# A shorter softplus chain and a new written order in a one-core hybrid decoder layer

## The chip, the cores and the metric

The kernel runs on one core of a Trainium2 chip. The metric is the device time of one execution in microseconds (us). A core has a matmul engine (PE; PEld is its weight load), a vector engine (DVE), an activation engine (ACT), GpSimd (POOL), and DMA queues, of which SP's carries the plain loads and stores and POOL's the accumulating ones. SBUF is the working memory, PSUM the memory that matmuls write.

## The reference

One layer on x of 1024 tokens by 1024 channels, in float32. `h` is x after an RMS norm, scaled and shifted by a modulation vector `mod`; the product of `h` with W_in gives five groups of 1024 columns each. The core of it:

```python
mod = c_act @ mod_w[l] + mod_b[l]
shift, scale, gate = jnp.split(mod, 3, axis=-1)
h = rmsnorm(x, norm_g[l]) * (1.0 + scale[:, None, :]) + shift[:, None, :]
u = h @ w_in[l]
cv, cg, cs, lx, ls = jnp.split(u, [D_CONV, 2 * D_CONV, 3 * D_CONV, 3 * D_CONV + D_LRU], axis=-1)
v = cv * jax.nn.sigmoid(cg)
v = causal_depthwise_conv(v, dw_w[l], dw_b[l])           # 31 taps
v = jax.nn.silu(layernorm(v, cln_g[l], cln_b[l]))
y_conv = (v @ pw2_w[l] + pw2_b[l]) * jax.nn.silu(cs)
xs = causal_depthwise_conv(lx, sc_w[l], sc_b[l])         # 4 taps
r = sigmoid(xs @ wr + br); i = sigmoid(xs @ wi + bi)     # block-diagonal, 8 heads
log_a = -LRU_C * r * jax.nn.softplus(-lam[l])
a = jnp.exp(log_a)
hs = linear_scan(a, jnp.sqrt(-jnp.expm1(2.0 * log_a)) * (i * xs))
y_lru = hs * jax.nn.silu(ls)
x = rmsnorm(x + (1.0 + gate) * (concat(y_conv, y_lru) @ w_out[l]), final_g)
```

The softplus of `lam` is a vector of 1024 numbers, held as 128 x 8. The `exp`, `tanh` and `sqrt` steps of every head's gates need it, from head 0 on.

## The kernel before

Everything is kept with channels on the 128 partitions and the 1024 tokens along a row, so a tile is 128 x 1024. A float32 operand is split into two rounded parts, `hi` and `lo` (in names: `uh`/`ul` for the input, `whi`/`wlo` for weights, `yh`/`yl` for the results y), and a product is three matmul passes, hi by hi, lo by hi and hi by lo. `whi` is an ACT cast of the loaded `raw`; `wlo` is `raw - whi`, made on DVE, on POOL or by an accumulating DMA.

W_in is worked off in column blocks of 128, called slots and numbered n. A slot n is 48 matmuls of 128 x 512 (8 row blocks k, 3 passes, 2 halves) into a PSUM tile `ps<n>`; there are three such tiles, taken in turn, so a slot can begin when the tile of three before has been read. What a slot computes is given by the string ORDER: `i4` is a CG or CV block and so on, `g1` the six-matmul gate products of head 1 (`gate1_0`, `gate1_1`), `i28+i36` a pair of blocks done together with fewer products (`up`, `dn`). Behind a slot its tile is read out: CG by a sigmoid on ACT (`sig`), CV by a product with `sig` on DVE (`v`, line 561), CS by a SiLU on ACT (`scs`, then stored to DRAM), LS by a SiLU on ACT (`sls`), LX by four taps on ACT and DVE (`xs`). `gates(i, n)` (from line 1419) turns the gate products into `r` and `g`, `a`, the scan `r` and the result `sls<i>*r`, which is y of the head. It is split at once or, for heads in the list YSP, stored to DRAM (`yd`) and fetched again (`yr`) ahead of the products that use it.

The 31 taps of the convolution run as fillers: on DVE for most tiles (`cacc`, `caccs`, sums in PSUM), as ACT products added by POOL's DMAs for tiles 1 and 3 (`cq`, `co`, `es`, `oo`). The pair slots need sums and differences of the input blocks, made on POOL (`hx`, `hls`). `modw` steps on DVE multiply a modulation weight by the silu of c and sum it.

Behind the slots come the first products with W_out (`lp`, `lx`, `ly` and so on, from the y of the lru heads), the layer norm, the products with pw2, the rest of W_out, the final norm and the stores. `lp0` is the first that reads `yh5` and `yl5`.

The order of the instructions on each engine is fixed when the program is built. A class Plan takes every operation with a priority and an estimated cost, plays the engines against each other with the limits of buffers, and writes down the order in which it would start them. The numbers at the top of the file (SPP the priority of the softplus, YRES the buffers kept back for fetches, PYM and PXL and others the heads whose products are given to POOL) and the table TURNS, which shifts single operations by a few units, set that order. On the chip each engine works its list strictly from the front.

`softplus8` (from line 1213) evaluates softplus as a series: with s = u / (u + 2) the logarithm's odd series is a polynomial in s2 = s * s, built from the highest term by a product (TT, line 561) and an addition (TS, line 575) for each term. Its eight-column steps have the name `sp_q`.

Of the kernel before, what the change touches and what calls it, by code (L numbers as in the profile page):

```python
# [14 lines left out]
P = 128  # L15
D = 1024
T = 1024
# [17 lines left out]
ORDER = "i10 i24 i2 g0 i25 i11 i3 i26 i12 i33 i4 g1 i34 i23 g2 i13 i35 i5 i27 g3 i21 i14 i39 i6 i28+i36 i15 i30+i38 i7 i29+i37 g5 i31 g4 i19 i18+i22 g7 g6 i20"  # L35
# [46 lines left out]
SPN = 40  # L82
# [10 lines left out]
DUOA = 3  # L93
DUOW = "big"
YSP = (0, 1, 2, 3)
YRES = 5
TSP = 24
# [3 lines left out]
DENG = {15: ("POOL", "DVE", "DMA"), 16: ("DVE", "DMA", "POOL"), 17: ("DMA", "DMA", "DVE"), 18: ("DMA", "DMA", "POOL"), 20: ("DMA", "DVE", "POOL"), 21: ("DVE", "POOL", "DVE"), 23: ("POOL", "POOL", "DMA"), 24: ("DMA", "DVE", "POOL"), 27: ("POOL", "DMA", "POOL"), 29: ("DMA", "DMA", "POOL"), 30: ("DVE", "DVE", "DVE"), 31: ("POOL", "DMA", "DVE"), 32: ("POOL", "POOL", "DMA"), 34: ("DMA", "DVE", "DVE"), 35: ("POOL", "POOL", "DVE"), 39: ("DVE", "POOL", "DVE"), 41: ("POOL", "DMA", "POOL")}  # L101
YDMA = (1, 3, 4, 6, 7)
EVD = 0
DUOE = 0.6
# [8 lines left out]
YSTEP = 0.3  # L113
LTD = (2,1)
PREN = 5
PRES = 4
PREP = 18
XCP = 17
PLAND = 8.0
XCN = 28  # L120
XCS = 1
LEV = ()
LWB = "big"
LWO = 0.7
FINP = -0.5
# [8 lines left out]
FORKN = -200  # L134
# [5 lines left out]
LSN = 2  # L140
# [8 lines left out]
LRV = (0, 1, 2, 3, 4, 6)  # L149
# [13 lines left out]
SPP = 35  # L163
# [5 lines left out]
WE = {5: "POOL", 6: "DMA", 7: "DVE", 8: "POOL", 10: "DVE", 11: "POOL", 12: "POOL", 14: "DMA", 18: "DVE", 19: "DVE", 20: "DVE", 23: "DVE", 24: "DVE", 25: "POOL", 26: "DVE", 27: "DVE", 28: "DMA", 30: "POOL", 32: "DMA", 34: "POOL", 35: "DVE", 37: "DVE", 38: "DVE", 39: "DMA", 41: "DMA"}  # L169
PDIRECT = (0, 2, 5, 6)  # L170
D1S = {19: -1.35, 21: -0.3, 32: -1.35, 33: 0.0, 35: -1.35, 36: -1.35, 38: 0.0, 39: -1.35, 40: 0.0, 41: -1.35}
PGM, PYM, PXL, PYL, PXR = (2, 3, 7), (4,), (0,), (1, 4), (4, 6)
# [19 lines left out]
    ("ACT", "c3", "es3", 0): 2,  # L192
    ("ACT", "graw3", "ghi3", 0): 0.9,
    ("ACT", "graw6", "ghi6", 0): -4,
    ("ACT", "raw36", "whi36", 0): -5.7,
    ("ACT", "rawpw21_0", "whipw21", 0): 2.6,
    ("ACT", "v1", "co1_12", 0): -5.4,
    ("ACT", "v3", "co3_4", 0): 0.7,
    ("ACT", "v6", "caccs6", 0): -0.1,
    ("ACT", "wz37", "wsh37", 0): 2,  # L200
    ("DVE", "c3", "mean", 0): -2.3,
    ("DVE", "c3", "vt1", 0): -2,
    ("DVE", "c3", "vu1", 0): 1,
    ("DVE", "c6", "mean", 0): -0.9,
    ("DVE", "c6", "vla3", 0): 1.1,
    ("DVE", "c6", "vu3", 0): 7.1,
    ("DVE", "c7", "lnbc", 0): 2.6,
    ("DVE", "cr1", "mean", 0): -1.9,
    ("DVE", "cr1", "vlb0", 0): 1.7,
    ("DVE", "cr1", "vt0", 0): 2.1,  # L210
    ("DVE", "cr2", "mean", 0): -5.5,
    ("DVE", "cr4", "lnbc", 0): 2,
    ("DVE", "vu1", "vla1", 0): 2.3,
    ("DVE", "yu0", "ylT40", 0): 0.3,
    ("PE", "fhi6", "first0", 2): 4,
    ("PE", "ghi6", "gate6_1", 0): -2,
    ("PE", "h34pw21", "xpw2_1", 7): 1.8,
    ("PE", "h34pw21", "ypw2_1", 0): -0.2,
    ("PE", "h34pw21", "ypw2_1", 1): -0.2,
    ("PE", "h34pw21", "ypw2_1", 2): -0.2,  # L220
    ("PE", "hlpw21", "xpw2_1", 0): 2,
    ("PE", "hlpw22", "xpw2_2", 0): 0.2,
    ("PE", "lsh3", "ld3", 0): 1.7,
    ("PE", "lsh3", "lx3", 2): -0.3,
    ("PE", "lsh3", "lx3", 3): -0.3,
    ("PE", "whi18", "ps18", 0): -1.2,
# [24 lines left out]
    ("PE", "whipw20", "xpw2_0", 1): 0.2,
    ("PE", "whipw20", "xpw2_0", 2): 5.2,
# [237 lines left out]
def hymba_layer(ctx: ExitStack, tc: tile.TileContext, xT, vecs, mod_w, w_first, w_in,  # L490
# [1041 lines left out]
    def acc_store(n, m, t):  # L1532
        ADD(n + 0.5, lambda: acc_d[m], t, r=[t, ("accd", m)], w=[("accd", m)], flight=LAND)
# [193 lines left out]
    def duo(m0, m1, n):  # L1727
# [14 lines left out]
        for to, (a, ai, ak), (b, bi, bk) , op in (  # L1742
# [4 lines left out]
            TT(q, CSUB, block(z, to), block(a, ai), block(b, bi), op, w_, r=ak + bk, w=[(z, to)],  # L1747
# [92 lines left out]
    def after_start(n):  # L1840
# [8 lines left out]
        if 0 <= (n - XCN) // XCS < KT and (n - XCN) % XCS == 0:  # L1849
            x_copy((n - XCN) // XCS, [started[n]])  # L1850
# [291 lines left out]
```

## Time and profile before

| | us |
|---|---|
| three runs | 729.41, 724.18, 729.10 |
| median | 729.1 |
| profiled execution | 728.72 |
| its span, first to last instruction | 726.7 |

| engine | busy us | share of the span |
|---|---|---|
| PE | 713.7 | 98% |
| PEld | 594.0 | 82% |
| DVE | 651.4 | 90% |
| ACT | 477.8 | 66% |
| POOL | 218.8 | 30% |

The profiled execution is 2.02 us longer than its span; a sum made from the trace's rows is set against 728.72. In the timelines a row gives the start, the duration, the engine, the line and the names with their numbers left out, and in brackets the idle time ahead of it and what ended it. Consecutive alike instructions are drawn together (x2). Rows of one engine overlap by their pipeline, so the cost of an instruction is the distance between starts.

### The profile page before, as it was taken

To read this page: it belongs to the slowest core of one execution; us is meant where nothing else is said; L and a number is where in the kernel's file an instruction comes from. 1 tells how busy PE (TensorE), PEld (TensorE's weight loads), DVE (VectorE), ACT (ScalarE), POOL (GpSimd) and SP (SyncE) were. 2 spreads that over 40 slices of the span, in tenths; PEclk is the share of its full clock that TensorE was granted. 3 is DMA by queue.
4 is the path that set the end of the run, shared out by engine and by line. 5 is a ranking of instruction groups with operands and counts; after the bars stand their busy time and mean duration, and the time that the engine had idled before them with its cause. 6 is when DMAs were issued, how large, how long until landed. Compare 5 with 4: busy or idle time off the path is not lost.

```text
span 726.7 us, 9084 instructions
## 1 busy us (share of the span) xinstructions
PE 713.7 (98%) x3244; PEld 594.0 (82%) x3244; DVE 651.4 (90%) x890; ACT 477.8 (66%) x604; POOL 218.8 (30%) x189
## 2 busy tenths in 40 slices
PE   9999999999979999999999999999999999999995
PEld 8888888888868888888888888878888888888885
DVE  7989999999999989989989999798799765998747
ACT  7650687868766693984694879946697644755322
POOL 0023334533676642463254262200101101010001
PEclk9999999999989999999999999999999999999999
DMA  9936357997976989879946328996838745783106
GB/s 345 407 143 191 56 154 199 229 259 173 194 171 165 235 228 243 203 184 250 221 121 198 86 72 218 268 303 157 223 82 194 205 104 130 230 228 128 52 1 231
DMA packets 45052, 135.95 MB, mean 187 GB/s; under 512 B 5088, under 2 KB 14560, under 8 KB 44896
## 3 DMA queue, kind: packets, MB, share of 16 engines
q0 software_dynamic: 16848, 45.52, 35.2%
q1 hardware_dynamic: 27152, 88.95, 34.6%
q10 hardware_dynamic: 1008, 0.92, 0.4%
q8 instruction: 25, 0.41, 0.2%
q14 instruction: 19, 0.16, 0.1%
HBM read 83.17 MB, written 25.17 MB: 149 GB/s over the span
## 4 chain that ended last, share of the span: by engine, by line
PE 68%; DVE 22%; ACT 6%; issue 3%; POOL 1%; DVEq 0%; ACTq 0%
PE ps L694 21%; PE xpw L870 6%; PE xout L870 6%; PE first L1003 5%; DVE caccs L553 4%; PE ypw L870 3%; DVE cacc L553 3%; PE lx L1578 3%; PE dn L1778 2%; PE up L694 2%; DVE xs L553 2%; PE gate L1429 1%; PE zpw L870 1%; PE lx L694 1%; PE dn L694 1%
## 5 line engine op out<-in xcount | busy, mean ns | idle before, releaser
L694 PE MATMUL ps<-uh,whi 128*128 128x512 f32 x448 | 139.3, 392 | 4.2 <-DVE v L561 4.2
L694 PE MATMUL ps<-uh,wlo 128*128 128x512 f32 x448 | 138.8, 391 | 0.0
L694 PE MATMUL ps<-ul,whi 128*128 128x512 f32 x448 | 138.8, 391 | 0.0
L694 PEld LDWEIGHTS ps<-uh,whi 128*128 128x128 f32 x448 | 84.7, 190 | 22.2 <-issue 4.6
L694 PEld LDWEIGHTS ps<-ul,whi 128*128 128x128 f32 x448 | 84.7, 189 | 17.8
L694 PEld LDWEIGHTS ps<-uh,wlo 128*128 128x128 f32 x448 | 84.7, 189 | 17.7
L553 DVE SCALAR_TENSOR_TENSOR cacc<-v,V,cacc 128x511 f32<-128x511 f32 (+14 forms) x90 | 67.0, 744 | 0.4
L542 ACT ACT_TABLE_LOAD x47 | 60.3, 1283 | 9.6 <-DVE r L1441 7.8
L561 POOL TENSOR_TENSOR wlo<-raw,whi 128x1024 fp32r<-128x1024 f32 (+1 forms) x16 | 41.2, 2580 | 78.4 <-ACT whi L534 76.3
L553 DVE SCALAR_TENSOR_TENSOR caccs<-v,V,caccs 128x511 f32<-128x511 f32 (+6 forms) x84 | 62.6, 746 | 1.9 <-ACT caccs L542 0.7
L553 DVE SCALAR_TENSOR_TENSOR caccs<-c,wsum,caccs 128x511 f32<-128x511 f32 (+6 forms) x84 | 62.4, 742 | 0.5
L534 ACT CAST whi<-raw 128x1024 fp32r<-128x1024 f32 (+1 forms) x44 | 44.0, 1007 | 23.8 <-PE ps L694 11.4
L566 POOL DMA_DIRECT2D es<-cq x30 | 29.1, 970 | 44.9 <-DMA es<-cq 10.8
L553 DVE SCALAR_TENSOR_TENSOR modw<-modw,sc 128x1024 f32<-128x1024 f32 x23 | 34.1, 1485 | 0.0
L566 POOL DMA_DIRECT2D oo<-co x26 | 27.6, 1060 | 18.2 <-DMA oo<-co 5.0
L542 ACT ACTIVATE cq<-v,V 128x511 f32<-128x511 f32 (+14 forms) x30 | 21.3, 711 | 10.8 <-DVE v L561 4.2
L561 POOL TENSOR_TENSOR o<-fin,bc 128x256 f32<-128x256 f32 (+1 forms) x6 | 4.9, 830 | 70.8 <-ACT bc L534 70.8
L561 DVE TENSOR_TENSOR wlo<-raw,whi 128x1024 fp32r<-128x1024 f32 (+1 forms) x21 | 26.2, 1246 | 0.0
L566 POOL DMA_DIRECT2D lz<-in_w_out_dram x16 | 14.1, 996 | 37.1 <-ACT lz L542 29.8
L566 POOL DMA_DIRECT2D accd<-acc x8 | 7.3, 910 | 58.5 <-ACT acc L542 34.2
L542 ACT ACTIVATE finsq<-fin 128x512 f32<-128x512 f32 (+2 forms) x14 | 7.9, 570 | 23.1 <-DVE fin L553 15.4
L1441 DVE TENSOR_TENSOR_SCAN r<-a,xs 128x1024 f32<-128x1024 f32 x8 | 22.4, 2796 | 0.1
(525 smaller groups left out, 1937.5 us busy)
## 6 DMA issues: line engine op xcount, KB each, us to landing
raw<-in_w_in_dram SPq DMA_DIRECT2D x36, 512.0 KB, 4.2
modw<-in_mod_w_dram SPq DMA_DIRECT2D x24, 512.0 KB, 8.0
scsd<-scs SPq DMA_DIRECT2D x8, 512.0 KB, 3.1
raw<-in_w_out_dram SPq DMA_DIRECT2D x8, 512.0 KB, 4.6
accd<-acc POOLq DMA_DIRECT2D x8, 512.0 KB, 7.2
rawpw<-in_pw_dram SPq DMA_DIRECT2D x8, 512.0 KB, 4.8
scsr<-scsd SPq DMA_DIRECT2D x8, 512.0 KB, 5.1
rawout<-in_w_out_dram SPq DMA_DIRECT2D x8, 512.0 KB, 3.7
```

The source lines that it names most:

```text
L534: act.copy(out(), in_())
L542: act.activation(out=out(), in_=in_(), func=func, **kw)
L553: dve.scalar_tensor_tensor(out=out(), in0=in0(), scalar=scalar, in1=in1(), op0=op0, op1=op1, accum_out=accum)
L561: lambda: e.tensor_tensor(out=out(), in0=a(), in1=b(), op=op), prio, r, w,
L566: return S.op("POOL", ISSUE, lambda: pool.dma_start(out(), a(), accum_op=ALU.add), prio, r, w, lag=RATE * n / T, after=after, flight=flight)
L694: pe.matmul(ps()[:, a - off:b - off], k3(lhs)()[:, at, :], rhs[k]()[:, a:b], start=(k == first and lhs is wh and rhs is xh and (a - off) % ...
L870: pe.matmul(half(ps, 0)(), half(*lhs)()[:, j * P:j * P + P], half(*rhs)(), start=start and at == 0 and i == 0, stop=at == len(order) - 1 a ...
L1003: pe.matmul(ps()[:, a - off:b - off], fw_part(lhs, k, i * P, i * P + P)(), rhs()[:, a:b], start=k == 0 and lhs is wh and rhs is xh, stop=k ...
L1429: pe.matmul(ps()[:, c0:c1], lhs()[:, j, :], rhs()[:, c0:c1], start=st == 0, stop=st == 2)
L1441: S.op("DVE", 2.2, lambda: dve.tensor_tensor_scan(out=r(), data0=a(), data1=xs(), initial=0.0, op0=ALU.mult, op1=ALU.add), pr, [a, xs], [r])
L1578: pe.matmul(half(ps, h)(), lhs()[:, o:o + P], half(*rhs)(), start=begin and at == 0 and t == 0, stop=at == len(order) - 1 and t == len(ter ...
L1778: pe.matmul(half(ps, h)(), lhs()[:, o:o + P], half(rhs, z)(), start=begin and j == 0 and t == 0, stop=j == NJ - 1 and t == 2, skip_group_c ...
```

## The change

Three things are done together.

The softplus chain. The product and the addition of a term become one instruction, `(q + 1/n) * s2`, so fifteen steps become eight:

```diff
-        TS(pr, q, s2, 1.0 / 17.0, 1.0 / 15.0, ALU.mult, ALU.add, r=[s2], w=[q])
-        for n in (13, 11, 9, 7, 5, 3, 1):
-            TT(pr, "DVE", q, q, s2, ALU.mult, KT, r=[q, s2], w=[q])
-            TS(pr, q, q, 1.0 / n, None, ALU.add, r=[q], w=[q])
-        TT(pr, "DVE", q, q, s, ALU.mult, KT, r=[q, s], w=[q])
+        TS(pr, q, s2, 1.0 / 17.0, None, ALU.mult, r=[s2], w=[q])
+        for n in (15, 13, 11, 9, 7, 5, 3):
+            STT(pr, q, q, 1.0 / n, s2, ALU.add, ALU.mult, KT, r=[q, s2], w=[q])
+        STT(pr, q, q, 1.0, s, ALU.add, ALU.mult, KT, r=[q, s], w=[q])
...
-SPP = 35
+SPP = -20
```

The settings of the planner, cut to those that move something named here, and two lines for the table of turns:

```diff
-ORDER = "i10 i24 i2 g0 i25 i11 i3 i26 i12 i33 i4 g1 i34 i23 g2 i13 i35 i5 i27 g3 i21 i14 i39 i6 i28+i36 i15 i30+i38 i7 i29+i37 g5 i31 g4 i19 i18+i22 g7 g6 i20"
+ORDER = "i10 i24 i2 g0 i25 i11 i3 i26 i33 i12 i4 g1 i34 i23 g2 i13 i35 i5 i27 g3 i20 i14 i39 i6 i28+i36 i15 i30+i38 i7 i29+i37 g5 i31 g4 i19 i18+i22 g6 i21 g7"
...
-YSP = (0, 1, 2, 3)
+YSP = (0, 1, 2, 3, 5)
...
-LRV = (0, 1, 2, 3, 4, 6)
+LRV = (0, 1, 2, 3, 4, 5, 6)
...
-PGM, PYM, PXL, PYL, PXR = (2, 3, 7), (4,), (0,), (1, 4), (4, 6)
+PGM, PYM, PXL, PYL, PXR = (2, 3), (0, 4), (0,), (4, 6, 7), (4, 6)
...
-    ("PE", "whi18", "ps18", 0): -1.2,
...
+    ("DVE", "v4", "caccs4", 0): -0.6,
```

Of the new helpers and choices in the code (a reload of the input from DRAM for the pair slots, other engines for their sums, another way to keep x for the end) the settings leave all off. The entries of the table WE for slots 27, 31, 33, 34, 40 and 41 have no effect, since those are pair slots or products of W_out, which other tables govern.

In instructions: PE has the same matmuls. DVE has six rows fewer: the seven softplus steps, and sls0's product goes to POOL (PYM), while head 7's product of `g` and `xs` comes from POOL (PGM) and one `wlo` of 768 columns is more. ACT loads its tables twice less often. POOL has one DMA fewer. SP has two DMAs more: y of head 5 is stored and fetched (512 KB each). Two neighbouring slots, a CG block and an LS block, change places (slots 14 and 15).

The softplus steps, which stood one by one among the taps and the `xs` steps from 100 to 121 us of the profile, stand right behind the last `ul` products now, one between each two of `wlo7`, `glo0`, `glo1`, `wsum`, `c0` and `bias2`, ahead of nearly all taps.

The first place: DVE ahead of `v4`, the read-out of slot 16, near 206 us. Before:

```order
L553 SCALAR_TENSOR_TENSOR caccs2_1549<-v2_1197,V_80,caccs2_1549 128x500
L553 SCALAR_TENSOR_TENSOR caccs2_1549<-v2_1197,V_80,caccs2_1549 128x499
L553 SCALAR_TENSOR_TENSOR modw17_1765,macc_96<-modw17_1765,sc_175 128x1024
L561 TENSOR_TENSOR v4_1849<-ps16_1745,sig4_1679 128x1024
L561 TENSOR_TENSOR wlo18_1853<-raw18_1713,whi18_1838 128x1024
L561 TENSOR_TENSOR xs1_1314<-g1_1851,xs1_1314 128x1024
L561 TENSOR_TENSOR glo3_1889<-graw3_1007,ghi3_1864 128x256
L561 TENSOR_TENSOR xs1_1314<-xs1_1314,r1_1587 128x1024
```

and now:

```order
L606 SCALAR_TENSOR_TENSOR caccs2_1555<-v2_1206,V_80,caccs2_1555 128x500
L606 SCALAR_TENSOR_TENSOR caccs2_1555<-v2_1206,V_80,caccs2_1555 128x499
L614 TENSOR_TENSOR wlo18_1835<-raw18_1710,whi18_1829 128x1024
L606 SCALAR_TENSOR_TENSOR caccs2_1555<-v2_1206,V_80,caccs2_1555 128x498
L614 TENSOR_TENSOR v4_1860<-ps16_1741,sig4_1758 128x1024
L614 TENSOR_TENSOR xs1_1293<-g1_1845,xs1_1293 128x1024
L614 TENSOR_TENSOR glo3_1882<-graw3_1013,ghi3_1858 128x256
L614 TENSOR_TENSOR xs1_1293<-xs1_1293,r1_1580 128x1024
L606 SCALAR_TENSOR_TENSOR modw17_1797,macc_96<-modw17_1797,sc_176 128x1024
```

`modw17` has moved from ahead of `v4` to behind the products of xs1; `wlo18` and one more `caccs2` tap have moved ahead of `v4`.

The second place: PE behind gate1_1. `ps17` and `ps18` are slots 17 and 18; `ps18` takes over the PSUM tile that `v4` reads. Before:

```order
L694 MATMUL ps17_1842<-uh2_275,whi17_1752 128x512 x2
L694 MATMUL ps17_1842<-ul2_284,whi17_1752 128x512 x2
L694 MATMUL ps17_1842<-uh2_275,wlo17_1767 128x512 x2
L694 MATMUL ps18_1878<-uh0_189,whi18_1838 128x512 x2
L694 MATMUL ps18_1878<-ul0_206,whi18_1838 128x512 x2
L694 MATMUL ps18_1878<-uh0_189,wlo18_1853 128x512 x2
```

and now, fifteen rows further on:

```order
L747 MATMUL ps17_1838<-uh7_488,whi17_1748 128x512 x2
L747 MATMUL ps17_1838<-ul7_507,whi17_1748 128x512 x2
L747 MATMUL ps17_1838<-uh7_488,wlo17_1760 128x512 x2
L747 MATMUL ps18_1928<-uh0_190,whi18_1829 128x512 x2
L747 MATMUL ps18_1928<-ul0_207,whi18_1829 128x512 x2
L747 MATMUL ps18_1928<-uh0_190,wlo18_1835 128x512 x2
```

Before, ps17 stops after three of its eight row blocks and ps18 comes in, whole, ahead of the other five. Now ps17 is done whole and then ps18: 15 rows of two matmuls that stood behind ps18 stand ahead of it.

The third place: SP's queue where the results y come back. `scsd` is the store of a `scs`, `lsh` and `lsl` are weight parts for the products of W_out. Before:

```order
L580 DMA scsd3_131<-scs3_3632 128x1024
L580 DMA lsh0_3714<-lsdh0_107 128x1024
L580 DMA yr0_3735<-yd0_117 128x1024
L580 DMA lsl0_3746<-lsdl0_108 128x1024
L580 DMA yr1_3755<-yd1_118 128x1024
L580 DMA yr2_3767<-yd2_120 128x1024
L580 DMA scsd2_132<-scs2_3772 128x1024
L580 DMA yr3_3814<-yd3_121 128x1024
L580 DMA raw42_3825<-in_w_out_dram 128x1024
```

and now:

```order
L633 DMA scsd3_132<-scs3_3621 128x1024
L633 DMA yd5_130<-sls5_3438 128x1024
L633 DMA yr0_3704<-yd0_117 128x1024
L633 DMA yr1_3726<-yd1_118 128x1024
L633 DMA yr2_3738<-yd2_120 128x1024
L633 DMA yr3_3767<-yd3_121 128x1024
L633 DMA scsd2_133<-scs2_3756 128x1024
L633 DMA yr5_3797<-yd5_130 128x1024
L633 DMA lsh0_3812<-lsdh0_107 128x1024
L633 DMA lsl0_3847<-lsdl0_108 128x1024
```

The store of y5 goes in ahead of the four older fetches, and its fetch stands behind the store of scs2, ahead of lsh0 and lsl0. On ACT the cast `yh5` moves from the place right behind head 7's gates to behind the casts of the other fetched results, and on DVE `yl5` follows behind `yls00` and `yls10`, whose two products stand earlier than before.

More of the change, by code (lines that the diff above doesn't have):

```diff
@@ L121 @@
 XCS = 1
+XADD = False
+XADDP = -1.0
+TSRC = "POOL"
+HSP = 2.0
+TSUBS = ("POOL",) * 8
+TLO = ("POOL",) * 4
+CENG = {21: "DVE", 17: "DVE", 36: "DVE", 33: "POOL", 22: "POOL", 15: "POOL", 16: "POOL"}
 LEV = ()
 LWB = "big"
-LWO = 0.7
-FINP = -0.5
+LWO = 0.3
+FINP = 0
 BCLATE = False
@@ L205 @@
[L205 to L214, printed above, removed]
+    ("ACT", "c1", "cq1_14", 0): -8,
+    ("ACT", "c3", "vhb1", 0): -1.7,
+    ("ACT", "cr0", "cr0", 0): 0.1,
+    ("ACT", "cr4", "vha2", 0): 1.8,
@@ new lines @@
+    ("ACT", "dn30", "sls6", 0): -4,
+    ("ACT", "ps17", "sls2", 0): -2,
+    ("ACT", "ps18", "scs7", 0): 0.2,
+    ("ACT", "raw36", "whi36", 0): -5.7,
+    ("ACT", "v1", "cq1_9", 0): 6.8,
+    ("ACT", "v6", "caccs6", 0): -0.5,
+    ("ACT", "vt0", "vhc0", 0): 4,
+    ("ACT", "vt2", "vhc2", 0): -1,
+    ("ACT", "vu1", "vha1", 0): -0.5,
+    ("ACT", "vu2", "vha2", 0): -1.9,
+    ("ACT", "yc5", "yhb2", 0): 3.7,
+    ("ACT", "yh4", "yl4", 0): -5.7,
+    ("ACT", "yhc1", "ylc1", 0): 1,
+    ("ACT", "yt2", "yhc2", 0): 2,
@@ L1532, in acc_store @@
     def acc_store(n, m, t):
+        if XADD:
+            acc_d[m] = dram.tile([P, T], F32, tag=f"acc{m}", name=f"accd{m}")
+            DMA(n + 0.5, lambda: acc_d[m], t, FULL_BYTES, r=[t], w=[("accd", m)])
+            return
         ADD(n + 0.5, lambda: acc_d[m], t, r=[t, ("accd", m)], w=[("accd", m)], flight=LAND)
```

199 lines of the change are left out of this document (131 added, 68 removed).

## The prediction

> **What bounds the kernel now.** I read the page's head and busy shares first, then the waits of the matmul engine, then its timeline where the one long wait is, then the windows round it, and last what VectorE and GpSimd did there. The page, and the waits of PE (engine waited for, us in total, times, longest):
>
> ```profile
> span 726.7 us, 9084 instructions
> PE 713.7 (98%) x3244; PEld 594.0 (82%) x3244; DVE 651.4 (90%) x890; ACT 477.8 (66%) x604; POOL 218.8 (30%) x189
> ...
> PE ps L694 <- DVE v L561: 4.2, 1, 4.2
> PE lx L1578 <- DVE yls L561: 0.3, 1, 0.3
> ```
>
> PE is busy for 98% and sets the time; DVE at 90% matters only where PE waits for it. Behind the opening PE has one wait of weight: 4.2 us, for the product `v`; the next one in size for DVE is the 0.3 us at lx. Its timeline there (start, duration, x2 is a pair of matmuls):
>
> ```profile
> 207.44 0.62 PE L694 MATMUL ps<-ul,whi 128*128 128x512 f32 x2
> 207.90 0.61 PE L694 MATMUL ps<-uh,wlo 128*128 128x512 f32 x2
> 212.69 1.19 PE L694 MATMUL ps<-uh,whi 128*128 128x512 f32 x2 [4.18 <-DVE v L561]
> 213.69 1.05 PE L694 MATMUL ps<-ul,whi 128*128 128x512 f32 x2
> ...
> 217.95 0.80 PE L694 MATMUL ps<-uh,whi 128*128 128x512 f32 x2
> 218.59 0.63 PE L694 MATMUL ps<-ul,whi 128*128 128x512 f32 x2
> ```
>
> Pairs normally start 0.4515 us apart (443 matmuls in 100 us in the window from 300 to 400, below; 207.44 to 207.90 here). The pair after 207.90 was due at 208.35 and started at 212.69: 4.34 lost. From 212.69 to 218.59 seven steps take 5.90 us where 3.16 would do: 2.74 more, since from 213.69 to 217.95 the pairs run 0.85 apart, near half pace. Together **7.08 us**. The windows (length, then busy time of PE, PEld, DVE, ACT and POOL with counts, granted clock, DMA share, GB/s) show that nothing else of the middle is lost:
>
> ```profile
> 200.00:213.00 13.00, 8.82 (x39) 7.06 (x38) 12.72 (x13) 6.47 (x9) 10.31 (x9) 0.94 0.71 151
> 213.00:235.00 22.00, 22.00 (x87) 17.89 (x87) 21.93 (x18) 14.50 (x20) 13.98 (x10) 0.88 0.62 182
> 235.00:300.00 65.00, 65.00 (x289) 53.81 (x288) 62.79 (x83) 45.20 (x55) 29.72 (x28) 1.00 0.98 228
> 300.00:400.00 100.00, 100.00 (x443) 82.81 (x442) 91.99 (x115) 71.82 (x87) 45.59 (x38) 1.00 0.80 195
> 400.00:480.00 80.00, 80.00 (x354) 65.88 (x352) 74.07 (x84) 69.18 (x70) 25.27 (x18) 1.00 0.64 168
> ```
>
> The granted clock is below 1.00 only round the wait. Why `v` came late, on DVE and POOL:
>
> ```profile
> 195.09 1.22 DVE L553 SCALAR_TENSOR_TENSOR modw<-modw,sc 128x1024 f32<-128x1024 f32 x1
> ...
> 196.23 10.16 DVE L553 SCALAR_TENSOR_TENSOR caccs<-v,V,caccs 128x511 f32<-128x511 f32 x13
> 206.29 5.11 DVE L553 SCALAR_TENSOR_TENSOR modw<-modw,sc 128x1024 f32<-128x1024 f32 x1
> ...
> 211.34 1.21 DVE L561 TENSOR_TENSOR v<-ps,sig 128x1024 f32<-128x1024 f32 x1
> 212.47 1.21 DVE L561 TENSOR_TENSOR wlo<-raw,whi 128x1024 fp32r<-128x1024 f32 x1
> 213.60 1.21 DVE L561 TENSOR_TENSOR xs<-g,xs 128x1024 f32<-128x1024 f32 x1
> ```
> ```profile
> 205.80 3.30 POOL L561 TENSOR_TENSOR hls<-hx,hhs 128x1024 fp32r<-128x1024 f32 x1
> 208.16 2.16 POOL L561 TENSOR_TENSOR hx<-hx 128x512 f32<-128x512 f32 x1
> ```
>
> The same `modw` form takes 1.22 at 195.09 and 5.11 at 206.29, where it runs beside two GpSimd products back to back (205.80 to 210.32). `v4` stands right behind it and ps18 needs the PSUM tile that `v4` reads. The 13 `caccs`, one of whose operands is in PSUM, take 0.77 each (10.06 us) although GpSimd was busy for 10.31 of the 13 us from 200 on: no hold to be seen.
>
> **The change, part by part.** *ps17 before ps18.* The 30 matmuls of ps17 that stood behind ps18 now stand ahead of it: 15 pairs by 0.4515 = 6.77 us. ps18 becomes due at 208.35 + 6.77 = 215.12. The row of `v` ends 0.14 ahead of PE's start (212.55, 212.69), so `v4` must start by 215.12 − 0.14 − 1.21 = 213.77. Were `v4` as late as now (211.34), PE would still not wait, by 2.4 us.
>
> *When v4 starts.* Ahead of it go: modw17 (5.05 with its hold, 206.29 to 211.34; 1.14 without, 195.09 to 196.23), the product sls0, which GpSimd now makes, and seven softplus steps. Ahead of it come wlo18 (1.13, 212.47 to 213.60) and one `caccs` (0.77). The rows of sls0 and of a softplus step, a held one beside a free one:
>
> ```profile
> 142.33 2.20 DVE L561 TENSOR_TENSOR sls<-sls,r 128x1024 f32<-128x1024 f32 x1
> ...
> 100.70 0.17 DVE L561 TENSOR_TENSOR sp_q<-sp_q,sp_s 128x8 f32<-128x8 f32 x1
> 100.77 0.69 DVE L561 TENSOR_TENSOR c<-v 128x512 f32<-128x512 f32 x1
> ...
> 102.17 2.10 DVE L561 TENSOR_TENSOR sp_q<-sp_q,sp_s 128x8 f32<-128x8 f32 x1
> 104.19 0.74 DVE L553 SCALAR_TENSOR_TENSOR cacc<-v,V,cacc 128x510 f32<-128x510 f32 x1
> ```
> ```profile
> 101.84 2.40 POOL L561 TENSOR_TENSOR wlo<-raw,whi 128x1024 fp32r<-128x1024 f32 x1 [2.26 <-ACT whi L534]
> ```
>
> The product at 142.33 is sls0: 2.1 of DVE's time held, where a same-sized one is free in 1.13 (212.47 to 213.60); a softplus step takes 0.07 from start to start, so seven give 0.5. Early end: 211.34 − 5.05 − 2.1 − 0.5 + 1.90 = 205.6. Late end, with each hold falling on whatever stands there instead: 211.34 − 1.14 − 1.13 − 0.5 + 1.90 = 210.5. I take the late end, since GpSimd's products stand in nearly the same row as before and wlo18 reads two SBUF tiles like modw17. Either end is ahead of 213.77, the late one by 3.3, so the wait goes whole: **−7.08**. modw17 itself moves behind `v4`, where its 1.14 to 5.05 us delay xs1 and the taps, which no matmul of the next stretch awaits closely.
>
> The Trainium skill ("GPSIMD Engine Reference", section 1, Specifications) says that GpSimd shares its SBUF interfaces with VectorE and that instructions with two SBUF inputs contend. The rows agree: 5.11 against 1.22 for `modw`, no hold for `caccs`. It speaks against the new order on DVE, where wlo18 merely inherits the hold of modw17; by it `v4` starts at the late end and the sum stays.
>
> *Softplus.* Eight steps in place of fifteen, now right behind the `ul` products and ahead of most of the taps. Two of the steps were held: 102.17 to 104.19 is 2.02, beside POOL's wlo from 101.84; and
>
> ```profile
> 110.73 2.28 DVE L575 TENSOR_SCALAR sp_q<-sp_q 128x8 f32<-128x8 f32 x1
> 112.92 0.74 DVE L553 SCALAR_TENSOR_TENSOR caccs<-c,wsum,caccs 128x510 f32<-128x510 f32 x1
> ```
>
> is 2.19. The chain now ends near 102, so the first hold may stay for one step. It is worth 0.5 to 4.6 us to DVE; to PE nothing, because the waits show none of PE for DVE in that stretch, and the taps behind the chain are fillers.
>
> *The spill of y5.* Stored and fetched again instead of kept. Cast and subtract now read the fetched tile, and lp0 needs them:
>
> ```profile
> 461.53 0.37 SPq L580 DMA_DIRECT2D yr<-yd  x1
> ```
> ```profile
> yr<-yd SPq DMA_DIRECT2D x4, 512.0 KB, 5.8
> ```
> ```profile
> 460.05 1.03 ACT L542 ACTIVATE scs<-up 128x1024 f32<-128x1024 f32 x1
> ...
> 466.95 1.05 ACT L534 CAST yh<-yr 128x1024 fp32r<-128x1024 f32 x1
> 467.91 1.04 ACT L534 CAST yhs<-yr 128x1024 fp32r<-128x1024 f32 x1
> ```
> ```profile
> 471.82 0.61 PE L694 MATMUL lp<-yh,whi 128*128 128x512 f32 x2
> 472.28 0.62 PE L694 MATMUL lp<-yl,whi 128*128 128x512 f32 x2
> ```
>
> The last fetch was issued at 461.53, behind the store of scs2; y5's now stands in that place, and lands about 5.8 later, at 467.3. On ACT eleven steps now stand between scs2 (done at 461.0) and its cast: nine of a cast's size at 0.96 (466.95 to 467.91) and two half-length ones of at most 0.74 (the half-length tap at 104.19), about 10.1 in all. So the cast runs from 471.1 to 472.1, and the subtract, of 1.2 like the product at 212.47, ends near 473.4 on DVE. In the new order lp0 reads y5 three matmuls later, at about 472.5 and 473.0. So 0 to 1 us of wait; I take 0.4. Against it the 0.3 us that lx waited for yls (in the waits above) goes, since its subtract is issued earlier. Net **+0.1**. The store itself stands behind scs3's in SP's queue and ahead of the four older fetches: only its issue, 0.4 like the fetch's, delays them.
>
> *All else* (two table loads fewer on ACT, products moved between DVE and POOL, the turns in the last products) moves work on engines with slack: from 235 to 480 DVE has 2.2 + 8.0 + 5.9 = 16.1 us idle, so it can follow a PE that is 7 us earlier. One row shows it: at its next `v` DVE waited for PE.
>
> ```profile
> 268.68 1.23 DVE L561 TENSOR_TENSOR v<-ps,sig 128x1024 f32<-128x1024 f32 x1 [1.79 <-PE ps L694]
> ```
>
> If that cover is gone, PE meets a new wait (below). The profiled execution took 728.72 (span 726.7 and 2.0 round it), 0.4 below the median of the runs shown, 729.1. Sum: 728.72 − 7.08 + 0.1 = **721.7**.
>
> **Rivals.** *Small waits take the place of the large one* (0.27). For it: a second hold like that of `r`, where one product took 6.34 instead of some 1.14 while GpSimd ran its products,
>
> ```profile
> 183.19 6.34 DVE L553 SCALAR_TENSOR_TENSOR r<-a,r 128x1024 f32<-128x1024 f32 x1
> ```
>
> would put `v4` at 210.5 + 5.2 = 215.7 and let PE wait 1.9; y5's full 1 us is as likely; and gate2_1 needs the tile that scs7 reads: six pairs, 2.7 us, lie between ps18's end and gate2_1, in which ACT must do a cast and scs7, 2.0, with 0.7 to spare. One to three of them: 722.6 to 726.5. At half pace each wait would cost up to 2.7 more. The Trainium skill ("TensorE: Matmul & The Clock Gate", Part 1, What's actually happening) has the clock halved after an idle window of some 3.4 us; by it waits of 1 or 2 us cost only themselves. The trace agrees as far as it goes: its wait of 4.34 is longer than that and was followed by half pace; a wait of 1 or 2 us it does not show.
>
> *The wait stays or comes back in another place* (0.10): DVE is the bound that PE only touches at `v4`, and being 7 us earlier PE runs into `v5` or `v6` instead. Against it stand the 16.1 us of idle time and the 1.79 above. It gives 726.5 to 729.5; it is also what results if the softplus and DVE edits do not do what they say and the new PE order is undone by a later `v4`.
>
> *Slower: lp0 waits for y5* (0.08). The fetch stands behind scs2's store in one queue, and the cast in ACT's; if scs2, which the up/dn slots feed, comes late, both come late, and PE stands at lp0. The price is the wait, and 2.7 more at half pace when it is as long as the 4.34 of now. A wait of 4.4 us brings back 7.1: the subtract would have to end 4.4 after 473.0, at 477.4, some 4 us later than I work out. From there it is slower than now; at 8 us, 721.3 + 8 + 2.7 = 732. What speaks against it is that the up/dn slot of scs2 hangs on PE alone, and PE is early, not late. Over 736.4 I give 0.03.
>
> **How the numbers follow.** The forecast, no wait over 1 us at v4 and lp0, gets 0.55, with 720.6 to 722.6: half a microsecond either side for the 0 to 1 at lp0 and the 0.4 between profile and median. The range that holds 8 in 10 takes in the small waits and a little of the third case: 720.6 to 727.5. A measurement of this kernel tells about 1% from no change, and its three runs spread over 0.7%. One per cent under 729.1 is 721.8, just above the forecast: two thirds of 0.55 lie below it, 0.37. Slower by over 1%, over 736.4: 0.03. Within: 0.60.
>
> **What would show it.** The row of `v4` with no wait of PE at ps18 and the granted clock 1.00 from 200 to 235 (first step); modw17 held behind `v4` or wlo18 held ahead of it (the hold only moved); the softplus steps at 0.07 each (second); lp0 without a wait for `yl` (third). A PE wait over 3 us with half pace anywhere, or DVE idle time gone between 235 and 480, would prove me wrong.

## The result and the profile after

The changed kernel took 722.33 us in the median of 11 runs (721.33 to 724.13), the kernel before 727.28 in 11 runs beside it (722.62 to 729.41). The ratio is 0.995, with an interval of 0.9926 to 0.9973: faster by half a per cent. The medians are 0.7% apart, because the times of the kernel before lie in two groups (four runs at 722.62 to 724.18, seven at 726.79 to 729.41). The profiled execution took 722.32, of which 720.5 are its span. The page's head and PE's waits after the change:

```profile
span 720.5 us, 9054 instructions
PE 710.7 (99%) x3244; PEld 591.5 (82%) x3244; DVE 642.2 (89%) x884; ACT 475.4 (66%) x601; POOL 217.9 (30%) x188
...
PE token_stats L1013 <- DVE ones L664: 1.1, 1, 1.1
PE lx L1640 <- ACT acc L595: 0.4, 1, 0.4
PE xout L923 <- DMA wloout<-in_w_out_dram: 0.4, 1, 0.4
PE dn L1851 <- DVE dn L614: 0.4, 1, 0.4
PE dn L1851 <- ACT up L587: 0.3, 1, 0.3
```

The wait of 4.2 us for `v` is gone, and so is the 0.3 of lx for yls; four waits of 0.3 to 0.4 are new. The windows round the old wait (busy PE, PEld, DVE, ACT, POOL, granted clock) show PE busy throughout at full clock:

```profile
200.00:213.00 13.00, 13.00 (x59) 10.78 (x58) 11.18 (x9) 6.54 (x9) 10.31 (x7) 1.00 0.99 218
213.00:235.00 22.00, 22.00 (x98) 18.22 (x98) 22.00 (x28) 17.59 (x20) 11.41 (x9) 1.00 0.73 193
```

DVE and then POOL there:

```profile
203.27 1.23 DVE L614 TENSOR_TENSOR wlo<-raw,whi 128x1024 fp32r<-128x1024 f32 x1 [1.71 <-ACT whi L587]
...
205.18 1.22 DVE L614 TENSOR_TENSOR v<-ps,sig 128x1024 f32<-128x1024 f32 x1
...
209.20 4.13 DVE L614 TENSOR_TENSOR xs<-xs,r 128x1024 f32<-128x1024 f32 x1
213.26 1.21 DVE L606 SCALAR_TENSOR_TENSOR modw<-modw,sc 128x1024 f32<-128x1024 f32 x1
```
```profile
206.73 2.27 POOL L614 TENSOR_TENSOR hx<-hx 128x512 f32<-128x512 f32 x1
208.94 0.87 POOL L619 DMA_DIRECT2D oo<-co  x1
209.55 2.70 POOL L614 TENSOR_TENSOR hx<-uh,ul 128x1024 f32<-128x1024 f32 x1
```

wlo18 is not held (1.23), `v4` starts at 205.18, and a hold now falls behind it, on the second product of xs1 (4.13 in place of 1.21), where PE does not feel it.

Where the time went is told by the start of the same matmul, counted from the first, in the two profiles:

| matmul no. | before | after | difference | what lies between |
|---|---|---|---|---|
| 60 | 13.12 | 12.60 | −0.52 | the opening, which differs between executions (matmul 60 starts at 13.37 in a second profile of the kernel before, below) |
| 900 | 198.38 | 197.86 | −0.52 | nothing |
| 960 | 219.05 | 211.46 | −7.59 | the wait for v4 and the half pace: −7.07 |
| 1620 | 368.66 | 362.39 | −6.28 | the two waits of `dn`, with the slower pairs beside them: +1.32 |
| 2160 | 491.96 | 484.88 | −7.08 | lx no longer waits for yls: −0.87; lp0 for yl5: +0.09 |
| 2280 | 519.16 | 512.79 | −6.36 | lx waits for acc: +0.72 |
| 2880 | 651.60 | 645.93 | −5.67 | xout waits for wloout: +0.70 |
| 3243, the last | 719.52 | 713.59 | −5.93 | small differences |

The span is 6.1 shorter and the execution 6.4, while the medians differ by 4.95. The rest of the difference is in the kernel before, which does not always take the course that its profile showed; the experiments came to that.

### The profile page after: what moved, and what is told of

Same layout as the page of the kernel before. It is cut to its first block, busy times and chain, and to the rows that moved or that the text cites. A ratio compares the mean times of both kernels' runs of the same rounds, so it can differ in the third digit from the quotient of the medians.

```text
span 720.5 us, 9054 instructions
## 1 busy us (share of the span) xinstructions
PE 710.7 (99%) x3244; PEld 591.5 (82%) x3244; DVE 642.2 (89%) x884; ACT 475.4 (66%) x601; POOL 217.9 (30%) x188
## 4 chain that ended last, share of the span: by engine, by line
PE 84%; DVE 7%; ACT 3%; issue 3%; POOL 2%; DMA 1%; DVEq 0%; POOLq 0%; ACTq 0%
PE ps L747 36%; PE xout L923 5%; PE first L1056 5%; PE xpw L923 5%; PE dn L747 3%; PE lx L1640 3%; PE dn L1851 3%; PE gate L1487 2%; PE ypw L923 2%; PE up L747 2%; DVE caccs L606 1%; PE y L893 1%; DMA wloout<-in_w_out_dram 1%; PE zout L923 1%; PE lx L747 1%
## 5 line engine op out<-in xcount | busy, mean ns | idle before, releaser
L614 POOL TENSOR_TENSOR wlo<-raw,whi 128x1024 fp32r<-128x1024 f32 (+1 forms) x16 | 38.6, 2416 | 71.8 <-ACT whi L587 70.1
L606 DVE SCALAR_TENSOR_TENSOR modw<-modw,sc 128x1024 f32<-128x1024 f32 x23 | 32.4, 1412 | 0.2 <-DMA modw<-in_mod_w_dram 0.2
L614 DVE TENSOR_TENSOR wlo<-raw,whi 128x1024 fp32r<-128x1024 f32 (+1 forms) x22 | 28.7, 1306 | 2.0 <-ACT whi L587 2.0
L619 POOL DMA_DIRECT2D oo<-co x26 | 26.1, 1067 | 14.4 <-issue 5.5
L606 DVE SCALAR_TENSOR_TENSOR xs<-ps,V,xs 128x1023 f32<-128x1023 f32 (+2 forms) x15 | 19.2, 1278 | 4.2 <-ACT xs L595 4.1
```

Source lines behind the costliest of these rows:

```text
L606: dve.scalar_tensor_tensor(out=out(), in0=in0(), scalar=scalar, in1=in1(), op0=op0, op1=op1, accum_out=accum)
L614: lambda: e.tensor_tensor(out=out(), in0=a(), in1=b(), op=op), prio, r, w,
L619: return S.op("POOL", ISSUE, lambda: pool.dma_start(out(), a(), accum_op=ALU.add), prio, r, w, lag=RATE * n / T, after=after, flight=flight)
```

## The experiments

In all but the softplus alone and the repeated profile, the order that the planner wrote was edited, by moving single operations in the finished list; every other instruction kept its place. Ratios are to the kernel before, with the 95% interval in brackets. `...` stands for the rest of an engine's list.

### The order on PE alone

```diff
 PE of the kernel before: gate1_1, ps17 blocks 0 to 2
+ps17 blocks 3 to 7
 ps18
-ps17 blocks 3 to 7
```

> The kernel before with one edit: the 30 matmuls of ps17 that stand behind ps18 stand ahead of it; DVE, ACT, POOL and SP as before. Theory A (the wait is one late read-out of v4, and 6.8 us of other matmuls ahead of ps18 cover it): v4 starts near 211.3 as now, modw17 still takes about 5.1, PE has no wait at ps18, the granted clock is 1.00 from 200 to 235, and the profiled time falls by 7.1 to about 721.6. Rival B (the gain of the change comes from DVE being earlier as a whole, by the softplus, sls0 and the moved products, and PE meets a late v5 or v6 without that): PE gets 7 us ahead and waits 1 to 5 us for a later read-out, time 723 to 727.

724.85 us in the median of 10 runs, ratio 1.0012 (0.9982 to 1.0043). Six runs lie at 722.72 to 725.35, four at 728.06 to 729.07; the profiled execution (728.06) is one of the four. PE's longest wait, and what it waited for on ACT:

```profile
PE ps L715 <- ACT sls L563: 4.7, 1, 4.7
...
231.01 1.03 ACT L555 CAST whi<-raw 128x1024 fp32r<-128x1024 f32 x1
231.94 1.01 ACT L563 ACTIVATE sls<-ps 128x1024 f32<-128x1024 f32 x1
```

There was no wait at ps18, as theory A had it, and PE was the full 7.07 us ahead there. But 14 us behind the start of ps18, ps19 needed the tile of ps17. That was ready at 215, while its read-out sls2 stands behind the next slots' casts on ACT, in the place that suited a ps17 that ends at 233. Neither theory had this: in this execution the place of sls2 in ACT's list took back what the order on PE had gained.

### v4 ahead of modw17 on DVE

```diff
 DVE of the kernel before: 13 caccs2
+v4
 modw17
-v4
 wlo18
```

> The kernel before with one edit: v4 stands ahead of modw17 on DVE, nothing else moves. Theory A: v4 starts when the taps end, at about 206.3, ps18 starts on time at 208.35, modw17 takes its 5 us behind v4, and the time falls by 7.1 to about 721.6. Rival C (what stands behind v4, modw17 with its hold and then xs1 and the scan of head 1, becomes what PE waits for): the wait moves to gate2 or ps19 and 2 to 5 us come back, 724 to 727.

725.84 us, ratio 0.9997 (0.9963 to 1.0031). Two of the 10 runs lie at 721.03 and 721.30, eight at 725.52 to 727.84; the profiled execution took 725.60.

```profile
PE ps L715 <- DVE wlo L582: 3.1, 1, 3.1
...
206.28 4.03 DVE L574 SCALAR_TENSOR_TENSOR modw<-modw,sc 128x1024 f32<-128x1024 f32 x1
210.23 1.22 DVE L582 TENSOR_TENSOR wlo<-raw,whi 128x1024 fp32r<-128x1024 f32 x1
```

`v4` came at 205.14 and ps18 began on time, but its third pair needs wlo18, which still stood behind the held modw17. The wait went on to the next product in the row; rival C had looked for it too far back.

### The shorter softplus alone

```diff
-TT q*s2, TS q+1/n (seven times), TT q*s
+STT (q+1/n)*s2 in the places of the TT, nothing in those of the TS, STT (q+1)*s
```

> The kernel before with the softplus alone shortened: each product takes the addition of its term along, at the places where the products stood, so DVE has seven instructions fewer and every order stays. Theory A: 0.07 us each, 0.5 us on DVE, none on PE; modw17 meets the same GpSimd products, so v4 starts at 210.8 to 211.4 and the time stays within 1 us of the kernel before. Rival D (the softplus, named first in the change, sets when DVE meets GpSimd's products): the two held steps (4.1 us) go too, DVE is 4 us early, the hold of modw17 falls elsewhere, and the time falls by 3 to 7.

726.81 us, ratio 1.0006 (0.9978 to 1.0034). One of the 10 runs lies at 721.61, nine at 725.36 to 728.23. The wait for `v` stayed, with 3.4 us in the profiled execution (725.36):

```profile
PE ps L715 <- DVE v L582: 3.4, 1, 3.4
...
211.00:218.00 7.00, 7.00 (x31) 5.55 (x30) 7.00 (x6) 5.38 (x9) 4.18 (x3) 1.00 0.88 243
```

Theory A held in the time: the seven instructions that the change is named for are, alone, worth nothing that can be measured. `v4` started at 209.36 and not at 210.8 to 211.4; of the 1.98 us against the first profile 1.16 is an earlier opening, and the rest was not traced. The second row, the window just behind the wait, is of interest below: this time no half pace followed.

### The changed kernel with PE's order undone

```diff
 PE of the changed kernel: gate1_1, ps17 blocks 0 to 2
+ps18
 ps17 blocks 3 to 7
-ps18
```

> The changed kernel with one edit undone: ps18 stands ahead of the last 30 matmuls of ps17 again, as before; all else as in the changed kernel. Theory A: v4 still starts near 205.2 and ends at 206.4, ahead of the 207.8 at which ps18 is then due, so there is no wait and the time is that of the changed kernel, within 0.5 us of 722.3. Rival E (the order on PE is what the change lives on): the wait comes back with 1 to 4 us, 723 to 729.

727.07 us, ratio to the kernel before 1.0015 (0.9991 to 1.0040); all ten runs lie between 725.59 and 728.57. PE's wait, ACT there, and the window behind it:

```profile
PE ps L768 <- ACT whi L608: 2.0, 1, 2.0
...
226.24 1.02 ACT L616 ACTIVATE sls<-ps 128x1024 f32<-128x1024 f32 x1 [6.58 <-PE ps L768]
227.16 1.04 ACT L608 CAST whi<-raw 128x1024 fp32r<-128x1024 f32 x1
...
228.50:236.00 7.50, 7.11 (x24) 5.30 (x24) 7.50 (x11) 7.47 (x10) 0.13 (x1) 0.77 1.00 240
```

The mirror of the first experiment, and theory A missed again: on ACT sls2 now stands ahead of whi19, so with a late ps17 ACT idles for 6.58 us and whi19 is late for ps19. A second wait of PE, 0.4 for scs7, follows.

### One block of ps17 instead of five

```diff
 PE of the kernel before: gate1_1, ps17 blocks 0 to 2
+ps17 block 3
 ps18
-ps17 block 3
 ps17 blocks 4 to 7
```

> The kernel before with one block of ps17 (6 matmuls, 1.35 us) moved ahead of ps18 instead of five. If v4 ends as in the profile of before, PE waits 3.0 in place of 4.3. If half pace sets in only behind a wait longer than some 3.4 us, the pairs behind it stay 0.45 apart and the profiled time falls by 1.35 + 2.7 = 4.1, to 724.6. If any wait of a few us halves the pace, it falls by 1.35 alone, to 727.4. The second group of times of the kernel before (722.6 to 724.2) would then be executions with such a shorter wait.

726.98 us in one run (the kernel before beside it: 728.10), close to the 727.4 of the second theory.

```profile
PE ps L715 <- DVE v L582: 2.8, 1, 2.8
...
213.00:220.00 7.00, 7.00 (x25) 5.58 (x25) 7.00 (x5) 4.58 (x8) 4.17 (x3) 0.76 0.87 229
```

The wait shrank as worked out, and half pace followed it all the same.

### GpSimd's two products away from modw17

```diff
 POOL of the kernel before: hx01 (with hx00), es1
-hls00, hx01
 oo1, oo3, hx10
+hls00, hx01
```

> The kernel before with the two GpSimd products that run beside modw17 (hls00 and the first hx01) moved behind the next accumulating DMAs and hx10 in GpSimd's list; PE, DVE, ACT and SP as before. Theory A (modw17 is held by those two products): modw17 takes 1.2 instead of 5.1, v4 starts at 207.4, PE waits about 0.4 at ps18, and the time falls by 6.5 to 7, to about 722. Rival F (modw17 takes 5.1 for another reason, such as its own accumulation or its load): it stays at 5.1 and the time at 728.7.

721.87 us in one run (the kernel before: 728.10).

```profile
202.62 1.22 DVE L574 SCALAR_TENSOR_TENSOR modw<-modw,sc 128x1024 f32<-128x1024 f32 x1
203.84 1.23 DVE L582 TENSOR_TENSOR v<-ps,sig 128x1024 f32<-128x1024 f32 x1
...
208.05 0.87 POOL L587 DMA_DIRECT2D oo<-co  x1 [5.91 <-ACT co L563]
```

modw17 takes 1.22 where GpSimd idles, as theory A had it. But it also starts at 202.62 and not at 206.29, though nothing ahead of it was changed. So this execution took another course before that, which the next one explains.

### The kernel before once more

> The kernel before, profiled once more. Its runs lie in two groups, 722.6 to 724.2 and 726.8 to 729.4. If this execution falls in the lower group, theory A expects the wait for v4 to be under 3 us or without the half pace behind it; the rival (the opening or the tail differs) expects the full 7.1 at v4 and the difference elsewhere. In the upper group it repeats the wait of 4.2.

The profiled execution took 724.09, in the lower group. The same instructions in the first profile of the kernel before (POOL alone; its `r` is in the prediction) and then in this one, POOL and DVE:

```profile
182.80 0.86 POOL L566 DMA_DIRECT2D es<-cq  x1 [4.31 <-issue]
183.37 2.72 POOL L561 TENSOR_TENSOR hx<-uh,ul 128x1024 f32<-128x1024 f32 x1
185.73 2.71 POOL L561 TENSOR_TENSOR wlo<-raw,whi 128x1024 fp32r<-128x1024 f32 x1
```
```profile
183.29 0.86 POOL L566 DMA_DIRECT2D es<-cq  x1 [4.78 <-ACT r L542]
183.86 2.83 POOL L561 TENSOR_TENSOR hx<-uh,ul 128x1024 f32<-128x1024 f32 x1
...
183.21 1.22 DVE L553 SCALAR_TENSOR_TENSOR r<-a,r 128x1024 f32<-128x1024 f32 x1
...
203.39 4.32 DVE L553 SCALAR_TENSOR_TENSOR modw<-modw,sc 128x1024 f32<-128x1024 f32 x1
207.64 1.21 DVE L561 TENSOR_TENSOR v<-ps,sig 128x1024 f32<-128x1024 f32 x1
...
PE ps L694 <- DVE v L561: 0.2, 1, 0.2
```

Up to the product `r` of head 1 the two executions run alike on DVE. Then `r` takes 6.34 us in the one (183.19) and 1.22 in the other (183.21): in the one, GpSimd's hx01 came 0.18 us behind its start and in the other 0.65. After that DVE is 5 us ahead, and still 2.9 when modw17 begins. modw17 is held again (4.32), but `v4` comes at 207.64 and PE waits 0.2. This execution is also the one to compare that of the experiment before with, as both have `r` free: modw17 takes 4.32 with GpSimd's two products beside it and 1.22 without them, so it is they that hold it. A race of half a microsecond, 25 us ahead of the wait, decides whether the kernel before pays some 4 us. It is not the whole 7.08: 0.7 of that stays at `v4`, and PE, now earlier, loses 1.5 in four steps of 0.2 to 0.4 up to matmul 1640.

### Both orders undone in the changed kernel

```diff
 PE of the changed kernel: gate1_1, ps17 blocks 0 to 2
+ps18
 ps17 blocks 3 to 7
-ps18
...
 DVE: wlo18, one caccs2
+modw17
 v4, xs1, glo3, xs1
-modw17
```

> The changed kernel with the two orders undone: ps18 ahead of the last 30 matmuls of ps17, and modw17 ahead of v4. Theory A: modw17 now starts at 205.2 beside the GpSimd products of 204.3 to 209.0 and takes 4 to 5; v4 starts at 209 to 210 and PE, due at 207.8, waits 2.5 to 3.5; the time is 725 to 729. Rival B (the earlier DVE alone is enough): no wait over 0.5, the time stays at 722.3.

726.56 us in one run. The row of `v4`, then the first pair of ps18 and, later on, the first two pairs of ps19:

```profile
207.57 1.21 DVE L635 TENSOR_TENSOR v<-ps,sig 128x1024 f32<-128x1024 f32 x1
```
```profile
207.62 0.61 PE L768 MATMUL ps<-uh,whi 128*128 128x512 f32 x2
...
227.51 0.73 PE L768 MATMUL ps<-uh,whi 128*128 128x512 f32 x2 [2.05 <-ACT whi L608]
228.08 0.63 PE L768 MATMUL ps<-ul,whi 128*128 128x512 f32 x2
```

ps18 started at 207.62, while `v4` was still reading its tile. So in the changed kernel ps18 does not take over that tile at all. The written programs say the same (first matmul of a slot, with the engines it waits for; before, then after):

```
ps18 <-uh0,whi18  waits DVE, Activation
ps19 <-uh0,whi19  waits Activation
...
ps18 <-uh0,whi18  waits Activation
ps19 <-uh0,whi19  waits DVE, Activation
```

With `v4` written behind the gate's read-out g1, ps18 gets the tile of gate1_1, and it is ps19, in the changed kernel 11 us behind the start of ps18, that needs `v4`'s. The wait for `v4` that theory A expected did not come, though modw17 took 2.79 ahead of it. The 2.05 us wait for whi19 is the fourth experiment's, and one of 1.6 for scs7 follows it.

### Out of the race: hx01 behind wlo16

```diff
 POOL of the kernel before: es3
-hx01
 wlo16
+hx01
 oo1
```

> The kernel before with one swap on GpSimd: the first hx01 behind wlo16 instead of ahead of it; all other lists as before. Theory T (the two groups of times of the kernel before are two courses, decided at 183 us, where the product r of head 1 on DVE starts within 0.2 us of hx01 on GpSimd: held for 6.3 us in one course, done in 1.2 in the other; held, v4 comes 4.2 us late and costs 7.1): wlo16 waits for its cast until 184.8, so r is always done in 1.2, PE waits at most 0.3 at ps18, and all runs lie in the lower group, 721.5 to 724.2, 0.3 to 0.6% under the kernel before. Rival G (the groups come from the opening, or the hold only moves to modw17 in full): the runs keep two groups, or all wait 2 to 4 us, and the median stays within 1 us of the kernel before.

723.92 us in 12 runs, all between 723.40 and 724.68; ratio 0.9965 (0.9944 to 0.9986). The 34 runs of the kernel before beside it lie at 722.63 to 724.04 (12 of them) and 725.46 to 729.23 (22).

```profile
182.59 1.22 DVE L574 SCALAR_TENSOR_TENSOR r<-a,r 128x1024 f32<-128x1024 f32 x1
...
184.19 2.40 POOL L582 TENSOR_TENSOR wlo<-raw,whi 128x1024 fp32r<-128x1024 f32 x1 [0.66 <-ACT whi L555]
...
PE ps L715 <- DVE v L582: 1.0, 1, 1.0
```

One swap on GpSimd, and the upper group is gone. Theory T is shown for the two groups; its wait of at most 0.3 was 1.0, as modw17 was still held. The profiles of the other edits that left GpSimd's list alone at this place agree with it. The two nearest to the turn are that of the second experiment (first two rows) and that of the next one:

```profile
181.83 6.55 DVE L574 SCALAR_TENSOR_TENSOR r<-a,r 128x1024 f32<-128x1024 f32 x1
182.23 2.71 POOL L582 TENSOR_TENSOR hx<-uh,ul 128x1024 f32<-128x1024 f32 x1
...
182.26 1.22 DVE L574 SCALAR_TENSOR_TENSOR r<-a,r 128x1024 f32<-128x1024 f32 x1
182.78 2.97 POOL L582 TENSOR_TENSOR hx<-uh,ul 128x1024 f32<-128x1024 f32 x1
```

`r` was held with hx01 0.18, 0.31, 0.34, 0.39 and 0.40 us behind its start, and free with 0.52, 0.64 and 0.65.

### modw17 behind v4 and wlo18

```diff
 DVE of the kernel before: 13 caccs2
-modw17
 v4, wlo18
+modw17
```

> The kernel before with modw17 moved on DVE behind both v4 and wlo18; nothing else moves. Theory T: with r held, v4 starts at 206.3 and wlo18 at 207.4, in time for 208.35 and 209.25, so PE has no wait at ps18 in either course; all runs 720.5 to 723, ratio 0.994 to 0.996 to the kernel before. Rival C (xs1, glo3 and the scan behind modw17 become late): a wait of 1 us or more at gate2 or ps19, and the runs keep an upper group.

725.87 us, ratio 0.9976 (0.9948 to 1.0004). Four of the 12 runs lie at 720.67 to 722.24, eight at 725.59 to 726.56. The profiled execution (721.04) was one of the four: no wait at ps18, `r` not held. That an upper group stays is rival C's sign, but the waits that it named are not in this profile. What the eight still pay, no profile caught; that it is the course with `r` held fits their share (the kernel before has 22 of 34), but is not shown.

### Three moves together

```diff
 POOL: hx01 behind wlo16; DVE: modw17 behind v4 and wlo18
...
 DVE near 485 us
-wlo42
 yls11
+wlo42
```

> The kernel before with three moves: hx01 behind wlo16 on GpSimd, modw17 behind v4 and wlo18 on DVE, and wlo42 behind yls11 on DVE at 485 us. Theory T: no wait for v4, and the 0.3 us wait of lx for yls (0.9 us with the slower pairs round it) goes too; it lacks the four small waits of the changed kernel (dn twice, lx for acc, xout for wloout, 2.7 us together), so it comes out 0.5 to 1.5 us under the changed kernel, at 720.8 to 721.8 in the median, ratio 0.992 to 0.995. Rival: wlo42 is late for lc1 by 1 us and takes that back.

722.77 us in 12 runs (721.84 to 724.42), ratio 0.9949 (0.9927 to 0.9971). No upper group, no wait for `v` or yls. That the eight of the experiment before are gone with hx01 out of the way speaks for the hold of `r` in them, though wlo42 was moved as well. It gives what the change gives, not more: its runs overlap with the changed kernel's, so it was not the better version that I expected. Its profiled execution, the longest of the twelve (724.42), waits 0.6 us at ps19 for sls2 and has an opening 1.4 us longer than the profile of the changed kernel.

### The changed kernel with PE's order undone and whi19 early

```diff
 PE of the changed kernel: gate1_1, ps17 blocks 0 to 2
+ps18
 ps17 blocks 3 to 7
-ps18
...
 ACT:
+whi19
 sls2
-whi19
```

> The changed kernel with ps18 ahead of the last 30 matmuls of ps17 again, and whi19 ahead of sls2 on ACT, as it stood before: the run with the order on PE undone alone waited 2.0 us for whi19, which stood behind sls2 and so behind the end of ps17. Theory T: without that, the order on PE is worth nothing, since v4 is ready at 206.4; time within 0.7 us of the changed kernel, 722 to 723.5. Rival E (ps17 first is needed): a wait of 1 us or more at ps18, ps19 or gate2_1 stays, 724 to 727.

728.79 us, ratio to the kernel before 1.0034 (1.0007 to 1.0062).

```profile
PE gate L1508 <- ACT scs L616: 3.3, 1, 3.3
...
232.00:240.00 8.00, 8.00 (x24) 6.33 (x25) 8.00 (x11) 6.19 (x7) 3.97 (x4) 0.65 0.86 257
```

The wait moved once more, to scs7, the read-out of ps18, which ACT's list has behind that of ps17. Rival E is right as far as this goes: with the lists that the changed kernel has on the other engines, ps17 has to come first. Moving scs7 as well was not tried.

## Why the prediction was right, and where not

**The figure.** 721.7 was forecast, 722.33 measured, inside the forecast's own 720.6 to 722.6. That the whole wait goes (−7.08) was right for the two profiled executions, where it came to −7.07. That the total fits to 0.6 is partly luck: new waits of 2.74 us were not in the sum, and an earlier opening (0.52), 0.9 more than forecast at lp0 and lx, and 0.7 behind xout and outside the span made up for most of them.

**What the sum was set against.** The step that failed is the start of the sum, 728.72, taken as if every execution of the kernel before paid the 7.08; the forecast of 721.7 against 729.1 was a gain of 7.4. The runs shown had 724.18 beside 729.41 and 729.10, and I took that for scatter. It was the other course: without the hold of `r`, the kernel before waits 0.2 us for `v4` (1.0 with hx01 moved). So the gain is 4.95 in the medians and 3.65 in the means (726.29 to 722.64), which is the ratio of 0.995. The 6.34 us row of `r` was quoted in the prediction, as a price for a second hold that might come; it was the first cause of the wait, and it could go.

**ps17 before ps18.** That PE would not wait even with `v4` "as late as now" held at ps18: in the first experiment `v4` started at 210.70 and PE did not wait there. As a gain it failed, since the edit alone only moved the wait to sls2 (4.7 us). And in the changed kernel ps18 did not need `v4` any more, so the deadline of 213.77 belonged to no wait. I took the tile from the order before; with `v4` behind g1 the tiles change hands in another order.

**When v4 starts.** I chose the late end, 210.5; it started at 205.18, ahead of the early end of 205.6 by about the earlier opening. Behind this is `r` again, which in the changed kernel starts 2.2 us before GpSimd's next product and takes 1.23. I had held that "GpSimd's products stand in nearly the same row as before". At this place they don't: the accumulating DMA es3, which stood ahead of hx01 and wlo16, stands behind both now, so hx01 ran at 173.36 and was done before `r` began. The new list is out of the race, as the swap of hx01 and wlo16 was:

```profile
180.12 1.23 DVE L606 SCALAR_TENSOR_TENSOR r<-a,r 128x1024 f32<-128x1024 f32 x1 [0.49 <-ACT r L595]
```
```profile
173.36 3.42 POOL L614 TENSOR_TENSOR hx<-uh,ul 128x1024 f32<-128x1024 f32 x1
182.33 2.41 POOL L614 TENSOR_TENSOR wlo<-raw,whi 128x1024 fp32r<-128x1024 f32 x1 [5.54 <-ACT whi L587]
```

The hold did not fall on wlo18, which GpSimd's list had spared that time (1.23).

**Softplus.** Nothing on PE, as forecast, and one hold left of two. DVE and POOL in the changed kernel:

```profile
101.37 2.58 DVE L606 SCALAR_TENSOR_TENSOR sp_q<-sp_q,sp_s 128x8 f32<-128x8 f32 x2
```
```profile
101.32 2.40 POOL L614 TENSOR_TENSOR wlo<-raw,whi 128x1024 fp32r<-128x1024 f32 x1 [1.37 <-ACT whi L587]
```

**y5.** Forecast +0.4 at lp0 and −0.3 at lx. lp0 lost 0.09: the subtract of y5 ended at 466.54 and its pair started at 466.65. lx gained 0.87, since the wait also slows the pairs beside it. The mechanism was right, the second term too small.

**All else.** "Moves work on engines with slack" was wrong by 2.74 us: `dn` twice, lx for acc and xout for wloout are new waits of 0.3 to 0.4, each costing 0.65 to 0.72 of PE's time. Being early does not bring them by itself: in the profile with modw17 behind `v4` and wlo18, PE gains 7.07 us on the first profile at the old wait and keeps them to the last matmul, and none of the four is there. So they come with the new order; with which part of it was not tried.

**Clock.** The rival that counted small waits without half pace leaned on a rule of the Trainium skill ("TensorE: Matmul & The Clock Gate", Part 1, What's actually happening): half clock after an idle window of some 3.4 us. The runs don't bear out that length as the condition (below): the wait of 2.0 us in the fourth experiment cost the clock, too, and one of 3.4 did not.

## What to carry to other kernels

Where the times of a kernel lie in two groups, profile it more than once before a change is priced: a race of half a microsecond between two engines, one of which holds up the other, can set the time of a wait far behind it. In a program whose engines each work a written list, an order on one engine has its value only with the lists of the others; undo or apply it alone, and the wait goes to the next instruction that was placed for it. And a buffer's next owner is read from the new program, not from the old one.

## What was not expected of the hardware

A wait of PE is followed by half pace or not, and its length does not tell which. Half pace followed waits of 2.0 us (fourth experiment: granted clock 0.77 in the window behind), 2.8 (0.76), 3.1 (second experiment: 0.72), 3.3 (0.65), 4.2 (the kernel before: pairs 0.85 apart) and 4.7 us (first experiment: 0.68); none followed 3.4 (1.00, the softplus alone). The same wait of 2.05 us for whi19 had it in the one kernel and not in the other (clock 1.00; pairs from 227.51 at 0.57 and 0.69, where half pace is 0.85). The Trainium skill ("TensorE: Matmul & The Clock Gate", Part 1, What's actually happening) calls the window in which idleness is counted free-running; that would make the same wait count or not by where it falls. No run here shows the window itself.

How hard DVE is held turns on less than a microsecond: `r` ran through in 1.22 when GpSimd's product started 0.52 us or more behind it, and with 0.40 or less it stood for 6.34 to 6.55, through that product and the next. These are the starts that the profile gives, in eight profiles; between 0.40 and 0.52 none fell.
